# A decoder step on one core: another order of the first loads, of the retrieval of token tiles and of the one-hot work, an earlier read-back, and a split last tile

## The chip, the core and the metric

The kernel runs on one core of a Trainium2 chip. It uses five engines: TensorE (PE, with its weight loads shown apart as PEld), VectorE (DVE), ScalarE (ACT), GpSimd (POOL) and SyncE (SP), which issues most of the DMAs. The metric is the device time of one execution in microseconds (us).

## What is computed

One layer of a decoder for 576 tokens: 512 of a prompt and 64 of a sample group, with 1024 features. A projection feeds windowed attention and a gated spatial branch, both are merged into the residual, then comes a mixture of 16,384 one-neuron experts with product-key retrieval, and a gate over a per-layer embedding.

```python
xn = _rms_norm(x, lp['attn_norm_g'])
z = xn @ lp['w_in']
...
x1 = x + h @ lp['w_out']
x2 = x1 + _peer(_rms_norm(x1, lp['ffn_norm_g']), lp['peer_w_q'], lp['peer_sub_keys'],
                lp['peer_u'], lp['peer_v'])
gate = jax.nn.sigmoid(_rms_norm(x2, lp['ple_norm_g']) @ lp['w_ple_gate'])
x3 = x2 + gate * (p_i @ lp['w_ple'])
...
# _peer, for each token: 8 heads, two halves of a query, top 16 of 128 keys in each half, top 16 of the 256 sums
idx = jnp.take_along_axis(cand_idx, pos, axis=-1)
gate = jax.nn.softmax(best, axis=-1)
act = jax.nn.gelu(jnp.einsum('thkd,td->thk', expert_u[idx], xb))
return jnp.einsum('thk,thkd->td', gate * act, expert_v[idx])
```

## The kernel before

All large products are made in fp32r with both operands split into a high and a low part, so that one block of a product is three matmuls. `split` makes the parts: the high one is an ACT copy (L66), the low one a DVE subtraction (L67). `load_block` reads a block of weights (512 KB), splits it, and gives the split a priority of 1000.

**Head.** `xT[k]`, k = 0 to 7, are the eight blocks of 128 features by 576 tokens. SP loads them, with the first block of `w_in` after the second of them. For each block ACT squares it (L140) and DVE adds the square up (L142), which serves the norm; ACT makes the scaled high part (L181) and DVE the low part (L182). `w_chunk(c, ...)` then multiplies a chunk of 128 columns of `w_in` (48 matmuls, for 256 and 320 tokens) and scales the result with the norm `rn`. The norm's sums over features come from small matmuls (L151, L165) in the same PE queue.

**The five tiles of tokens** are numbered 0 (the 64 sample tokens), 1 to 4 (128 prompt tokens each). `retrieve(ti)` is the top-16 search of one tile, mostly DVE work, a generator that yields between heads. Tiles 0 and 1 fetch their experts' rows from memory (**gather**: L707 on POOL, then DVE L719 and L726). Tiles 2, 3 and 4 (384 tokens) go through **all** experts instead:

- `stage1()` makes one of 128 columns of activations, 24 matmuls of 128x384 against `peer_uT` (L82). 19 of these columns (`SPILL`) are written to memory (`ad`).
- `build_g(tb)`, 24 blocks of 16 tokens, makes the gate of each token as a 128x128 matrix: for each token, a product of two one-hot matrices, `oa` (weights, L822's stationary side) and `ob` (the moving side, 128 columns), both 128x128 in fp32. Four tokens are a group. In even groups ACT makes `oa` and DVE `ob`, one operation of 128x512 (L813). In odd groups, here called mixed ones, DVE makes both: `oa` in one 128x512 compare (L816), `ob` in four operations of 128x128, compare and multiply in one (L819). There are 48 mixed groups. ACT copies the result out of PSUM, and it goes to memory (`gd`).
- `stage2` multiplies the gated activations with `peer_v`: 18 matmuls of 128x512 for each of the 128 columns (L939). Spilled columns are read back as `x1c` from a pool of three buffers, two columns ahead (L946), before DVE multiplies them with the gates (L974) and splits them (L66, L67).

**Order.** The program is written in one order and a scheduler lists each engine's instructions in it, moved by the priorities. SP issues its DMAs in its list's order. `S1_TOPK` says how many columns of stage 1 stand in the retrieval of each tile, `TBK` = 7 at which block of the build the retrieval has to be complete. Before, the tiles 0, 1, 2 are retrieved first, and 3 and 4 step by step inside the build, two steps for each block.

The time from 513.5 to 883.4 us, in which stage 1, the build and the end of retrieval run side by side, is called **phase one** here. Stage 2 follows it.

**Tail.** `finish_tile` makes the last gate of a tile of tokens: 48 matmuls of 128x512 (`tail_gate`, L902) into two PSUM banks that are finished together, then for each half a sigmoid on ACT (L909), a multiplication and an addition on DVE (L910, L911), and a store (`tail_out`).

Of the kernel before, what the change touches and what calls it, by code (L numbers as in the profile page):

```python
# [47 lines left out]
def tile_decoder_step(ctx: ExitStack, tc: tile.TileContext, a, o):  # L48
# [3 lines left out]
    def pool(stack, name, bufs, side="left", **kw):  # L52
        return stack.enter_context(tc.tile_pool(name=name, bufs=bufs, side=side, reuse_waits="tile", **kw))
# [6 lines left out]
    def cload(name, shape, pl=None):  # L60
        t = (pl or const).tile(shape, F32, name="c_" + name, bufs=1)
        S.dma_start(t, a[name])
        return t
# [2 lines left out]
        A.activation(hi, src, AF.Copy)  # L66
        V.tensor_sub(lo, src, hi.bitcast(F32))  # L67

    def load_block(src, shape=(P, KC, P)):
# [4 lines left out]
        with tc.high_priority(offset=1000):  # L74
            split(raw, hi, lo)
        return hi, lo

# [14 lines left out]
    def mm():  # L92
        return psM.tile([P, 512], F32, name="mm")
# [74 lines left out]

    vecs = cload("vecs", [P, 18])
    xT = f8(f4)  # L170
    for k in range(KC):
        S.dma_start(xT[k], a["xT"][k])
        if k == 1:
            first = load_block(a["w_in"][0])
    ident = cload("ident", [P, P])
    xn = (f8(x4), f8(x4))
    tot, add = sumsq()
    for k in range(KC):
        with tc.high_priority(offset=500):
            add(k, xT[k])  # L180
        A.activation(xn[0][k], xT[k], AF.Copy, scale=vecs[:, k:k + 1])  # L181
        V.scalar_tensor_tensor(xn[1][k], xT[k], vecs[:, k:k + 1], xn[0][k].bitcast(F32),  # L182
                               op0=ALU.mult, op1=ALU.subtract)
    rn = e1.tile([P, NT], F32, name="rn", bufs=1)
    with tc.high_priority(offset=500):
        for cols, ps in rstd_rows(tot, lambda: bank("sc")):
# [2 lines left out]
    def w_chunk(c, dst, out):  # L189
        def scaled(ps, cols):  # L190
            with tc.high_priority(offset=1000):
                V.tensor_tensor(dst[:, cols], ps, rn[:, cols], op=ALU.mult)
            out(cols)
        joint(load_block(a["w_in"][c]) if c else first, xn, scaled)

    kraw, vTr = tt(), tt()
    w_chunk(0, kraw, lambda cols: None)
# [584 lines left out]
    def make_ew(e0, e1_, gtf):  # L782
        pt = bank("pt")
        for q, src in enumerate((e1_, gtf, e0)):
            T.transpose(out=pt[:, q * P:(q + 1) * P], in_=src, identity=ident)
        ew = ep.tile([P, 4, P], F32, name="ew")
        A.activation(ew[:, 1:4, :], pt[:, 0:3 * P].rearrange("p (a b) -> p a b", a=3), AF.Copy)
        A.activation(ew[:, 0, :], pt[:, P:2 * P], AF.Copy, scale=-1.0)
        ewT.append(ew)

    found = {}
    tqs.close()
# [2 lines left out]
    ep = pool(gs_s, "ep", 2)  # L795
    op = pool(gs_s, "op", 2)
    gsp = [pool(gs_s, "gsp%d" % i, 1) for i in range(2)]

    def build_g(tb):
        ti, t0 = divmod(tb * TB, P)  # L800
        ew = ewT[ti]
        gs = gsp[(tb + 1) % 2].tile([P, NJ, TB], F32, name="gs")
        for t4 in range(0, TB, 4):
            pt = psB.tile([P, 512], F32, name=("sc", "pt")[t4 // 4 % 2])
            oa = op.tile([P, 4, P], F32, name="oa")
            ob = op.tile([P, 4, P], F32, name="ob")
            c = t0 + t4
            if (tb * TB + t4) // 4 % ONE[1] < ONE[0]:
                for t in range(4):
                    A.activation(oa[:, t, :], iota, AF.Abs, scale=-1.0, bias=ew[:, 3, c + t:c + t + 1])  # L810
                    A.activation(oa[:, t, :], oa[:, t, :], AF.Relu, scale=ew[:, 0, c + t:c + t + 1],
                                 bias=ew[:, 2, c + t:c + t + 1])
                V.tensor_tensor(ob, iota[:, None, :].to_broadcast([P, 4, P]),  # L813
                                ew[:, 1, c:c + 4][:, :, None].to_broadcast([P, 4, P]), op=ALU.is_equal)
            else:
                V.tensor_tensor(oa, iota[:, None, :].to_broadcast([P, 4, P]),  # L816
                                ew[:, 3, c:c + 4][:, :, None].to_broadcast([P, 4, P]), op=ALU.is_equal)
                for t in range(4):
                    V.tensor_scalar(ob[:, t, :], iota, ew[:, 1, c + t:c + t + 1], ew[:, 2, c + t:c + t + 1],  # L819
                                    op0=ALU.is_equal, op1=ALU.mult)  # L820
            for t in range(4):
                T.matmul(pt[:, t * P:(t + 1) * P], lhsT=oa[:, t, :], rhs=ob[:, t, :], start=True, stop=True)  # L822
            A.activation(gs[:, :, t4:t4 + 4], pt.rearrange("p (t j) -> p j t", t=4), AF.Copy)
        if tb == NB // TB - 1:
            A.activation(g0, gs[:, 0:JB, :], AF.Copy)
        S.dma_start(gd[:, :, tb].rearrange("c p j t -> p c (j t)"), gs.rearrange("p (c j) t -> p c (j t)", j=JB))

    for ti in range(3):
        for _ in retrieve(ti, ti < 2):
            if len(acts) < S1_TOPK[ti]:  # L830
                stage1()
        if ti == 0:
            steps.append(gather_steps())
        while len(acts) < S1_TOPK[ti]:
            stage1()
    phase[0] = 1
    rest_t = [retrieve(ti, False) for ti in (3, 4)]
    for tb in range(NB // TB):
        if tb == TBK:
            for i, r_ in enumerate(rest_t):  # L840
                for _ in r_:
                    pass
                make_ew(*found[5 - len(rest_t) + i])
            tks.close()
            late = pool(aLs, "aL", 1, "right")
            acp.append(late.tile([P, RING - NXP, NB], F32, name="aL"))
            g0 = late.tile([P, JB, TB], F32, name="g0")
        if tb < TBK:
            goal = S1_TOPK[2] + (tb + 1) * (S1_PRE - S1_TOPK[2]) // TBK
        else:  # L850
            goal = S1_PRE + (tb - TBK + 1) * (NSP + RING - 1 - S1_END - S1_PRE) // (NB // TB - TBK)
        while len(acts) < goal:
            stage1()
        if tb == 0:
            make_ew(*found[2])
# [49 lines left out]
    def tail_out(x2, r, c0, ps, sg, pl):
        S.dma_start(pl[:r], pld[c0:c0 + r])
        for hh in range(2):
            hs = slice(hh * 512, (hh + 1) * 512)
            A.activation(sg[:r, hs], ps[hh][:r], AF.Sigmoid)  # L909
# [219 lines left out]
```

## Time and profile before

| | us |
|---|---|
| three runs | 1780.88, 1782.16, 1788.48 |
| median | 1782.16 |
| profiled execution, its own time | 1776.88 |
| its span, first to last instruction | 1775.1 |
| PE busy in the span | 1744.3 |
| DVE busy | 1434.0 |
| ACT busy | 867.0 |

The span is what the trace covers; 1.8 us of the execution lie around it. The profiled execution is 5.3 us shorter than the median. PE is busy for 98% of the span, yet its matmuls are pipelined, so a busy PE may still take a longer step from one instruction to the next than it needs.

### The profile page before, as it was taken

To read this page: it belongs to the slowest core of one execution; us is meant where nothing else is said; L and a number is where in the kernel's file an instruction comes from. 1 tells how busy PE (TensorE), PEld (TensorE's weight loads), DVE (VectorE), ACT (ScalarE), POOL (GpSimd) and SP (SyncE) were. 2 spreads that over 40 slices of the span, in tenths; PEclk is the share of its full clock that TensorE was granted. 3 is DMA by queue.
4 is the path that set the end of the run, shared out by engine and by line. 5 is a ranking of instruction groups with operands and counts; after the bars stand their busy time and mean duration, and the time that the engine had idled before them with its cause. 6 is when DMAs were issued, how large, how long until landed. Compare 5 with 4: busy or idle time off the path is not lost.

```text
span 1775.1 us, 27763 instructions
## 1 busy us (share of the span) xinstructions
PE 1744.3 (98%) x10094; PEld 1575.1 (89%) x10094; DVE 1434.0 (81%) x2876; ACT 867.0 (49%) x1525; POOL 525.9 (30%) x390
## 2 busy tenths in 40 slices
PE   7999999999999899999999999999999999999998
PEld 7988999999999899999988887899899899887876
DVE  6455556548999999999898888998888888999862
ACT  6567444343236698999833333333333333333441
POOL 0000000000002112455245554454544554566300
PEclk9999999999999999999999999999999999999999
DMA  7211233443226577999999999999999999999741
GB/s 242 75 60 38 71 105 122 141 152 106 81 92 225 173 244 235 361 350 355 352 388 367 371 388 364 394 410 369 365 338 360 364 334 331 335 379 376 284 132 70
DMA packets 176457, 457.06 MB, mean 257 GB/s; under 512 B 15552, under 2 KB 76736, under 8 KB 174272
## 3 DMA queue, kind: packets, MB, share of 16 engines
q1 hardware_dynamic: 120736, 253.22, 40.6%
q0 software_dynamic: 55584, 202.07, 30.8%
q8 instruction: 79, 1.29, 0.3%
q14 instruction: 58, 0.48, 0.1%
HBM read 420.18 MB, written 35.78 MB: 257 GB/s over the span
## 4 chain that ended last, share of the span: by engine, by line
PE 77%; issue 7%; DVE 6%; DMA 5%; POOL 3%; ACT 1%; SPq 0%; DVEq 0%; POOLq 0%; ACTq 0%
PE mm L82 36%; PE oacc L939 21%; PE pv L82 5%; POOL row L707 3%; PE sc L822 2%; DMA row<-peer_v,idx 2%; PE pt L822 2%; PE oacc L902 2%; DVE w_lo L67 2%; PE sc L82 1%; DMA x1c<-ad 1%; DVE row L719 1%; DMA row<-peer_u,idx 1%; PE sc L580 1%; PE pv L447 1%
## 5 line engine op out<-in xcount | busy, mean ns | idle before, releaser
L66 ACT ACTIVATE w_hi<-w_raw 128x1024 fp32r<-128x1024 f32 x325 | 343.9, 1059 | 372.9 <-PE mm L82 287.1
L707 POOL DMA_INDIRECT row<-peer_u,idx x192 | 261.1, 1360 | 872.0 <-issue 520.8
L67 DVE TENSOR_TENSOR w_lo<-w_raw,w_hi 128x1024 fp32r<-128x1024 f32 x325 | 396.6, 1221 | 74.0 <-ACT w_hi L66 73.7
L82 PE MATMUL mm<-xd,w_hi 128*128 128x384 f32 x1552 | 405.9, 341 | 0.5 <-ACT w_hi L66 0.5
L82 PE MATMUL mm<-x,w_hi 128*128 128x256 f32 (+1 forms) x1600 | 329.7, 300 | 9.8 <-ACT x L181 9.5
L707 POOL DMA_INDIRECT row<-peer_v,idx x192 | 263.3, 1372 | 231.8 <-DVE acc L726 202.8
L82 PEld LDWEIGHTS mm<-xd,w_hi 128*128 128x128 f32 x1552 | 281.6, 189 | 5.9 <-ACT w_hi L66 0.8
L82 PEld LDWEIGHTS mm<-x,w_hi 128*128 128x128 f32 x1600 | 257.8, 190 | 24.1 <-ACT x L181 10.0
L82 PE MATMUL mm<-xd,w_lo 128*128 128x384 f32 x776 | 264.4, 341 | 3.7 <-DVE w_lo L67 3.7
L726 DVE SCALAR_TENSOR_TENSOR acc<-row,wts,acc 128x1024 f32<-128x1024 f32 x192 | 245.8, 1280 | 5.3 <-DMA row<-peer_v,idx 4.9
L939 PE MATMUL oacc<-w_hi,wl 128*128 128x512 f32 x768 | 242.0, 397 | 3.7 <-DVE wl L67 3.6
L939 PE MATMUL oacc<-w_lo,wh 128*128 128x512 f32 x768 | 242.0, 396 | 0.4 <-DVE w_lo L67 0.4
L939 PE MATMUL oacc<-w_hi,wh 128*128 128x512 f32 x768 | 242.3, 396 | 0.0
L719 DVE SCALAR_TENSOR_TENSOR row<-row,xr 128x1024 f32<-128x1024 f32 x192 | 231.6, 1221 | 11.0 <-DMA row<-peer_u,idx 8.6
L82 PE MATMUL mm<-x,w_lo 128*128 128x256 f32 (+1 forms) x800 | 236.6, 296 | 0.0
L939 PEld LDWEIGHTS oacc<-w_hi,wl 128*128 128x128 f32 x768 | 144.3, 188 | 39.6 <-DVE wl L67 5.5
L939 PEld LDWEIGHTS oacc<-w_lo,wh 128*128 128x128 f32 x768 | 144.4, 188 | 35.5 <-DVE w_lo L67 1.7
L939 PEld LDWEIGHTS oacc<-w_hi,wh 128*128 128x128 f32 x768 | 143.7, 188 | 29.4 <-ACT xr L921 0.8
L82 PEld LDWEIGHTS mm<-x,w_lo 128*128 128x128 f32 x800 | 151.7, 190 | 1.1 <-issue 0.8
L82 PEld LDWEIGHTS mm<-xd,w_lo 128*128 128x128 f32 x776 | 147.0, 189 | 4.7 <-DVE w_lo L67 4.7
L82 PE MATMUL pv<-xd,w_hi 128*128 128x384 f32 x496 | 136.7, 348 | 0.7 <-ACT x L776 0.7
L66 ACT ACTIVATE wh<-x 128x384 fp32r<-128x384 f32 x66 | 34.7, 526 | 162.6 <-PE oacc L939 153.1
(304 smaller groups left out, 2308.8 us busy)
## 6 DMA issues: line engine op xcount, KB each, us to landing
w_raw<-peer_uT SPq DMA_DIRECT2D x128, 512.0 KB
w_raw<-peer_v SPq DMA_DIRECT2D x128, 512.0 KB
gd<-gs SPq DMA_DIRECT2D x24, 1024.0 KB
gs<-gd SPq DMA_DIRECT2D x15, 1536.0 KB
w_raw<-w_in SPq DMA_DIRECT2D x30, 512.0 KB
w_raw<-peer_wq SPq DMA_DIRECT2D x16, 512.0 KB
w_raw<-w_br SPq DMA_DIRECT2D x8, 512.0 KB
w_raw<-w_out SPq DMA_DIRECT2D x8, 512.0 KB
```

What stands on the lines that cost most here:

```text
L66: A.activation(hi, src, AF.Copy)
L67: V.tensor_sub(lo, src, hi.bitcast(F32))
L82: mark_pe[0] = T.matmul(ps, lhsT=w[wi][:, wk + k, :], rhs=x[xi][k], start=i == 0, stop=i == n - 1)
L447: T.matmul(ps[:r], lhsT=xi[:, k, :r], rhs=wl_[k][wi][:, hh * 512:(hh + 1) * 512], start=i == 0, stop=i == 5)
L580: T.matmul(ps[:, b * P:(b + 1) * P], lhsT=qp[:, b * P:(b + 1) * P], rhs=sk, start=True, stop=True)
L707: ins = G.indirect_dma_start(out=row_, out_offset=None, in_=table, in_offset=bass.IndirectOffsetOnAxis(ap=ix, axis=0))
L719: V.scalar_tensor_tensor(row_, row_, 1.0, xrs[ti], op0=ALU.mult, op1=ALU.mult, accum_out=dots[:, s:s + 1])
L726: V.scalar_tensor_tensor(accs[ti], row_, wts[:, s:s + 1], accs[ti], op0=ALU.mult, op1=ALU.add)
L822: T.matmul(pt[:, t * P:(t + 1) * P], lhsT=oa[:, t, :], rhs=ob[:, t, :], start=True, stop=True)
L902: T.matmul(ps[hh][:r], lhsT=xi[:, k, :r], rhs=w[k][wi][:, hh * 512:(hh + 1) * 512], start=k == 0 and xi is xh and wi == 0, stop=k == KC - ...
L939: mark_pe[0] = T.matmul(oacc[t][hh], lhsT=wi[:, ts], rhs=vi[:, hh * 512:(hh + 1) * 512], start=j == 0 and last == 0 and vi is vh, stop=j = ...
```

## The change

Five parts. (a) Head: SP loads the first block of `w_in` ahead of the `xT` blocks and the second ahead of the constants; the high and low parts come ahead of the squares; the first chunk goes through k with both halves of the tokens in step, and the first three chunks use banks of three pools. (b) Tiles 0 and 2 are retrieved first, and 3, 1 and 4 inside the build, three steps for each block. (c) In a block of the build, one bf16 compare of 128x1024 (`hot`) serves both mixed groups, and one multiplication of 128x512 makes `ob` from it; in `ob` the four tokens are now innermost, so that the moving side of a matmul takes every fourth element. (d) `x1c` is read back four columns ahead instead of two, from the same three buffers. (e) The tail loads its embedding before the gate's matmuls, and the last tile is done in three groups of columns, 512, 256 and 256, each with its own output.

```diff
-S1_TOPK = (4, 9, 13)
+S1_TOPK = (4, 12)
...
 
     vecs = cload("vecs", [P, 18])
     xT = f8(f4)
+    first = [load_block(a["w_in"][0])]
     for k in range(KC):
         S.dma_start(xT[k], a["xT"][k])
-        if k == 1:
-            first = load_block(a["w_in"][0])
+    first.append(load_block(a["w_in"][1]))
     ident = cload("ident", [P, P])
+    first.append(load_block(a["w_in"][2], urgent=False))
     xn = (f8(x4), f8(x4))
     tot, add = sumsq()
     for k in range(KC):
-        with tc.high_priority(offset=500):
+        with tc.high_priority(offset=1500):
+            A.activation(xn[0][k], xT[k], AF.Copy, scale=vecs[:, k:k + 1])
+            V.scalar_tensor_tensor(xn[1][k], xT[k], vecs[:, k:k + 1], xn[0][k].bitcast(F32),
+                                   op0=ALU.mult, op1=ALU.subtract)
+    with tc.high_priority(offset=500):
+        for k in range(KC):
             add(k, xT[k])
-        A.activation(xn[0][k], xT[k], AF.Copy, scale=vecs[:, k:k + 1])
-        V.scalar_tensor_tensor(xn[1][k], xT[k], vecs[:, k:k + 1], xn[0][k].bitcast(F32),
-                               op0=ALU.mult, op1=ALU.subtract)
...
-        joint(load_block(a["w_in"][c]) if c else first, xn, scaled)
+        w = first[c] if c < 3 else load_block(a["w_in"][c])
+        if c:
+            joint(w, xn, scaled, bk=(mm, lambda: bank("pv"), lambda: bank("pt"))[c] if c < 3 else mm)
+            return
+        pss = [mm()[:, :cols.stop - cols.start] for cols in HALVES]
+        for k in range(KC):
+            for ps, cols in zip(pss, HALVES):
+                for i, (wi, xi) in enumerate(((0, 0), (0, 1), (1, 0))):
+                    T.matmul(ps, lhsT=w[wi][:, k, :], rhs=xn[xi][k][:, cols], start=k == 0 and i == 0,
+                             stop=k == KC - 1 and i == 2)
+        for ps, cols in zip(pss, HALVES):
+            scaled(ps, cols)
...
         ew = ep.tile([P, 4, P], F32, name="ew")
+        ewh = ep.tile([P, P], BF16, name="ewh")
+        A.activation(ewh, pt[:, 0:P], AF.Copy)
         A.activation(ew[:, 1:4, :], pt[:, 0:3 * P].rearrange("p (a b) -> p a b", a=3), AF.Copy)
         A.activation(ew[:, 0, :], pt[:, P:2 * P], AF.Copy, scale=-1.0)
-        ewT.append(ew)
+        ewT.append((ew, ewh))
...
+    hp = pool(gs_s, "hp", 1)
+    iota4 = hp.tile([P, P, 4], BF16, name="iota4")
+    A.activation(iota4, iota[:, :, None].to_broadcast([P, P, 4]), AF.Copy)
...
+        ew, ewh = ewT[ti]
+        hot = hp.tile([P, P, 2, 4], BF16, name="hot")
+        e1c = ewh[:, t0:t0 + TB].rearrange("p (g s t) -> p g s t", g=2, s=2)[:, :, 1, :]
+        V.tensor_tensor(hot, iota4[:, :, None, :].to_broadcast([P, P, 2, 4]),
+                        e1c[:, None].to_broadcast([P, P, 2, 4]), op=ALU.is_equal)
         gs = gsp[(tb + 1) % 2].tile([P, NJ, TB], F32, name="gs")
...
-            if (tb * TB + t4) // 4 % ONE[1] < ONE[0]:
+            cols = [ob[:, t, :] for t in range(4)]
+            if t4 // 4 % 2 == 0:
...
             else:
                 V.tensor_tensor(oa, iota[:, None, :].to_broadcast([P, 4, P]),
                                 ew[:, 3, c:c + 4][:, :, None].to_broadcast([P, 4, P]), op=ALU.is_equal)
-                for t in range(4):
-                    V.tensor_scalar(ob[:, t, :], iota, ew[:, 1, c + t:c + t + 1], ew[:, 2, c + t:c + t + 1],
-                                    op0=ALU.is_equal, op1=ALU.mult)
+                obx = ob.rearrange("p a b -> p (a b)").rearrange("p (x t) -> p x t", t=4)
+                V.tensor_tensor(obx, hot[:, :, t4 // 8, :],
+                                ew[:, 2, c:c + 4][:, None, :].to_broadcast([P, P, 4]), op=ALU.mult)
+                cols = [obx[:, :, t] for t in range(4)]
             for t in range(4):
-                T.matmul(pt[:, t * P:(t + 1) * P], lhsT=oa[:, t, :], rhs=ob[:, t, :], start=True, stop=True)
+                T.matmul(pt[:, t * P:(t + 1) * P], lhsT=oa[:, t, :], rhs=cols[t], start=True, stop=True)
...
-    for ti in range(3):
+    for i, ti in enumerate((0, 2)):
         for _ in retrieve(ti, ti < 2):
-            if len(acts) < S1_TOPK[ti]:
+            if len(acts) < S1_TOPK[i]:
                 stage1()
         if ti == 0:
             steps.append(gather_steps())
-        while len(acts) < S1_TOPK[ti]:
...
     phase[0] = 1
-    rest_t = [retrieve(ti, False) for ti in (3, 4)]
+    rest_t = [(ti, retrieve(ti, ti < 2)) for ti in (3, 1, 4)]
+
+    def rest_step():
+        if next(rest_t[0][1], 1) == 1:
+            ti, _ = rest_t.pop(0)
+            if ti in found:
+                make_ew(*found[ti])
+
...
         while len(acts) < goal:
+            if tb == 0 and len(acts) == goal - 1:
+                make_ew(*found[2])
             stage1()
-        if tb == 0:
-            make_ew(*found[2])
         build_g(tb)
-        for _ in range(2):
-            if rest_t and next(rest_t[0], 1) == 1:
-                rest_t.pop(0)
-                make_ew(*found[4 - len(rest_t)])
+        for _ in range(3):
+            if rest_t:
...
@@ -941,9 +967,10 @@
 
     tails, spp, back = [], [], {}
     for j in range(NJ):
-        if j + 2 in SPILL:
-            back[j + 2] = d3.tile([P, NB], F32, name="x1c")
-            S.dma_start(back[j + 2], ad[sorted(SPILL).index(j + 2)])
+        for jb in (2, 4) if j == 0 else (j + 4,):
+            if jb in SPILL:
+                back[jb] = d3.tile([P, NB], F32, name="x1c")
+                S.dma_start(back[jb], ad[sorted(SPILL).index(jb)])
...
     def finish_tile(i, x2, xh, xl, sg, r, c0):
-        tail_gate(ws, xh, xl, r, banks[i])
-        tail_out(x2, r, c0, banks[i], sg, tw.tile([P, D], F32, name="pl"))
+        pl = tw.tile([P, D], F32, name="pl")
+        S.dma_start(pl[:r], pld[c0:c0 + r])
+        parts = list(zip(banks[i], (slice(0, 512), slice(512, D))))
+        groups = [parts]
+        if i == 4:
+            groups = [parts[:1], [(banks[i][1], slice(512, 768))], [(banks[0][0], slice(768, D))]]
+        for g in groups:
+            tail_gate(ws, xh, xl, r, g)
+            tail_out(x2, r, c0, sg, pl, g)
```

SP, the start of the program: `vecs` are scale constants, `c_92` and `c_93` two buffers of four `xT` blocks each, `w_raw` a block of weights. Before, SP's list starts thus:

```order
L62 DMA c_vecs<-vecs 128x18
L172 DMA c_92<-xT 128x576 x2
L71 DMA w_raw<-w_in 128x1024
L172 DMA c_92<-xT 128x576 x2
L172 DMA c_93<-xT 128x576 x4
L62 DMA c_ident<-ident 128x128
```

The changed kernel, with its own line numbers, starts SP's list thus:

```order
L61 DMA c_vecs<-vecs 128x18
L70 DMA w_raw<-w_in 128x1024
L172 DMA c_92<-xT 128x576 x4
L172 DMA c_93<-xT 128x576 x4
L70 DMA w_raw<-w_in 128x1024
L61 DMA c_ident<-ident 128x128
L70 DMA w_raw<-w_in 128x1024
```

The first block of `w_in` has moved ahead of all eight `xT`, the second ahead of `ident`, and the third is in front of the other constants.

DVE, a block late in the build: `row,dots` are gather's dot products, `w_lo` a split of stage 1. Before, two mixed groups and an even one between them stand thus:

```order
L813 TENSOR_TENSOR ob<-c_iota,ew 128x512
L816 TENSOR_TENSOR oa<-c_iota,ew 128x512
L819 TENSOR_SCALAR ob<-c_iota,ew 128x128 x4
L719 SCALAR_TENSOR_TENSOR row,dots<-row,xr 128x1024 x3
L813 TENSOR_TENSOR ob<-c_iota,ew 128x512
L67 TENSOR_TENSOR w_lo<-w_raw,w_hi 128x1024
L816 TENSOR_TENSOR oa<-c_iota,ew 128x512
L819 TENSOR_SCALAR ob<-c_iota,ew 128x128 x4
```

After the change a whole block, two even and two mixed groups, stands thus:

```order
L822 TENSOR_TENSOR hot<-iota_5616,ewh 128x1024
L836 TENSOR_TENSOR ob<-c_iota,ew 128x512
L66 TENSOR_TENSOR w_lo<-w_raw,w_hi 128x1024
L839 TENSOR_TENSOR oa<-c_iota,ew 128x512
L842 TENSOR_TENSOR ob<-hot,ew 128x512
L732 SCALAR_TENSOR_TENSOR row,dots<-row,xr 128x1024 x2
L836 TENSOR_TENSOR ob<-c_iota,ew 128x512
L839 TENSOR_TENSOR oa<-c_iota,ew 128x512
L842 TENSOR_TENSOR ob<-hot,ew 128x512
```

The four operations of a mixed group's `ob` have become one, and one `hot` of 128x1024 stands at the start of a block.

SP, the start of stage 2: `gd` to `gs` is the read of gates, `peer_v` and `peer_uT` are weights. Before, the first read-backs stand thus:

```order
L946 DMA x1c<-ad 128x384 x2
L71 DMA w_raw<-peer_v 128x1024
L946 DMA x1c<-ad 128x384
L71 DMA w_raw<-peer_uT 128x1024
L966 DMA gs<-gd 128x3072
L71 DMA w_raw<-peer_v 128x1024 x2
L946 DMA x1c<-ad 128x384
L71 DMA w_raw<-peer_uT 128x1024
L966 DMA gs<-gd 128x3072
```

After the change they stand thus:

```order
L973 DMA x1c<-ad 128x384 x3
L70 DMA w_raw<-peer_v 128x1024 x2
L993 DMA gs<-gd 128x3072
L973 DMA x1c<-ad 128x384
L70 DMA w_raw<-peer_uT 128x1024
L70 DMA w_raw<-peer_v 128x1024 x2
L993 DMA gs<-gd 128x3072
L70 DMA w_raw<-peer_uT 128x1024
```

The third read-back now stands with the first two, and the fourth ahead of the next `peer_uT` block: each is one pair of columns earlier.

## Rows read from the trace of the kernel before

**Rows 1.** Page, part 1: busy time and share of the span.

```profile
PE 1744.3 (98%) x10094; PEld 1575.1 (89%) x10094; DVE 1434.0 (81%) x2876; ACT 867.0 (49%) x1525; POOL 525.9 (30%) x390
```

**Rows 2.** Stretches: window, length, busy us (count) of PE, PEld, DVE, ACT, POOL; clock, DMA.

```profile
544.00:690.00 146.00, 138.31 (x831) 133.66 (x830) 143.22 (x465) 110.65 (x206) 25.62 (x20) 0.98 0.71 226
690.00:875.00 185.00, 184.81 (x1230) 176.58 (x1230) 181.27 (x358) 170.75 (x409) 83.25 (x57) 1.00 1.01 346
1075.00:1150.00 75.00, 68.33 (x323) 57.23 (x323) 65.29 (x106) 23.69 (x32) 35.81 (x27) 1.00 0.97 377
```

**Rows 3.** Phase one, line L82 alone: busy PE and PEld, with counts.

```profile
513.50:883.40 369.90, 303.75 (x1507) 260.23 (x1507) 0.99 0.83 278
```

**Rows 4.** Phase one, line L822 alone, same columns.

```profile
513.50:883.40 369.90, 116.20 (x768) 102.90 (x768) 0.99 0.83 278
```

**Rows 5.** Chain in phase one: start us, length us, piece.

```profile
517.94 4.16 PE mm L82 x24
...
696.79 0.89 PE sc L822 x8
```

**Rows 6.** Timeline of DVE, build: start us, us, line, operation.

```profile
745.10 0.68 DVE L813 TENSOR_TENSOR ob<-c_iota,ew 128x512 f32<-128x512 f32 x1
745.71 0.68 DVE L816 TENSOR_TENSOR oa<-c_iota,ew 128x512 f32<-128x512 f32 x1
...
747.44 1.11 DVE L819 TENSOR_SCALAR ob<-c_iota,ew 128x128 f32<-128x128 f32 x4
748.46 0.69 DVE L813 TENSOR_TENSOR ob<-c_iota,ew 128x512 f32<-128x512 f32 x1
```

**Rows 7.** Timeline of DVE, retrieval.

```profile
558.81 1.22 DVE L67 TENSOR_TENSOR w_lo<-w_raw,w_hi 128x1024 fp32r<-128x1024 f32 x1
559.95 0.69 DVE L653 TENSOR_TENSOR l<-pr 128x1024 bf16<-128x1024 bf16 x1
560.55 0.29 DVE L681 TENSOR_REDUCE den<-gate 128x8 f32<-128x128 f32 x1
```

**Rows 8.** Timeline of PE, head.

```profile
9.18 1.44 PE L82 MATMUL mm<-x,w_hi 128*128 128x256 f32 x3 [9.18 <-ACT x L181]
...
12.38 0.41 PE L82 MATMUL mm<-x,w_lo 128*128 128x256 f32 x1
...
12.60 0.47 PE L82 MATMUL mm<-x,w_hi 128*128 128x320 f32 x1
```

**Rows 9.** Chain in the head: start us, length us, piece.

```profile
17.05 1.19 PE sc L151 x12
...
29.52 0.97 PE pv L216 x4
30.49 6.35 PE mm L82 x48
```

**Rows 10.** First 32 us, line L165 alone: busy PE and PEld, with counts.

```profile
0.00:32.00 32.00, 1.80 (x10) 1.46 (x10) 1.00 0.74 260
```

**Rows 11.** Tile x1c, 900 to 1140 us: DVE and ACT idle until (us, times).

```profile
  DMA x1c<-ad: 13.4, 7
```

**Rows 12.** Timeline around two waits in stage 2.

```profile
1081.44 0.56 DVE L974 TENSOR_TENSOR x1c<-x1c,gs 128x384 f32<-128x384 f32 x1 [4.91 <-DMA x1c<-ad]
...
1084.12 0.44 PE L82 MATMUL mm<-xd,w_lo 128*128 128x384 f32 x1 [2.49 <-DVE w_lo L67]
```

**Rows 13.** Timeline a little later.

```profile
1122.56 0.73 PE L939 MATMUL oacc<-w_hi,wl 128*128 128x512 f32 x2 [1.15 <-DVE wl L67]
```

**Rows 14.** Timeline of the end.

```profile
1768.34 0.63 PE L902 MATMUL oacc<-gh,x 128*128 128x512 f32 x2
1768.81 1.08 ACT L909 ACTIVATE xn<-oacc 128x512 f32<-128x512 f32 x2 [10.11 <-issue]
...
1770.65 1.29 DVE L911 TENSOR_TENSOR xn<-xn,x 128x512 f32<-128x512 f32 x2
```

More of the change, by code (lines that the diff above doesn't have):

```diff
@@ L31 @@
 GT = (2.0, 3.5)
-ONE = (1, 2)
 TAIL0 = 112
 TAIL1 = 122
-S1_TOPK = (4, 9, 13)
+S1_TOPK = (4, 12)
 TBK = 7
@@ L67, in split, with load_block @@
         V.tensor_sub(lo, src, hi.bitcast(F32))
-    def load_block(src, shape=(P, KC, P)):
+    def load_block(src, shape=(P, KC, P), urgent=True):
         raw = wp.tile(list(shape), F32, name="w_raw", bufs=4)
@@ L73, in load_block @@
         lo = wp.tile(list(shape), F32R, name="w_lo", bufs=3)
-        with tc.high_priority(offset=1000):
+        with tc.high_priority(offset=1000 if urgent else 0):
             split(raw, hi, lo)
@@ L797, in tile_decoder_step @@
     gsp = [pool(gs_s, "gsp%d" % i, 1) for i in range(2)]
+    hp = pool(gs_s, "hp", 1)
+    iota4 = hp.tile([P, P, 4], BF16, name="iota4")
+    A.activation(iota4, iota[:, :, None].to_broadcast([P, P, 4]), AF.Copy)
     def build_g(tb):
         ti, t0 = divmod(tb * TB, P)
-        ew = ewT[ti]
+        ew, ewh = ewT[ti]
[3 more added lines that the diff above has]
+                        e1c[:, None].to_broadcast([P, P, 2, 4]), op=ALU.is_equal)
         gs = gsp[(tb + 1) % 2].tile([P, NJ, TB], F32, name="gs")
@@ L833, in tile_decoder_step @@
             steps.append(gather_steps())
-        while len(acts) < S1_TOPK[ti]:
+        while len(acts) < S1_TOPK[i]:
             stage1()
     phase[0] = 1
-    rest_t = [retrieve(ti, False) for ti in (3, 4)]
+    rest_t = [(ti, retrieve(ti, ti < 2)) for ti in (3, 1, 4)]
[4 more added lines that the diff above has]
+                make_ew(*found[ti])
     for tb in range(NB // TB):
         if tb == TBK:
[L840 to L843, printed above, removed]
+            while rest_t:
+                rest_step()
             tks.close()
@@ L848, in tile_decoder_step @@
         if tb < TBK:
-            goal = S1_TOPK[2] + (tb + 1) * (S1_PRE - S1_TOPK[2]) // TBK
+            goal = S1_TOPK[1] + (tb + 1) * (S1_PRE - S1_TOPK[1]) // TBK
         else:
@@ L852, in tile_decoder_step @@
         while len(acts) < goal:
+            if tb == 0 and len(acts) == goal - 1:
+                make_ew(*found[2])
             stage1()
-        if tb == 0:
-            make_ew(*found[2])
         build_g(tb)
-        for _ in range(2):
-            if rest_t and next(rest_t[0], 1) == 1:
-                rest_t.pop(0)
-                make_ew(*found[4 - len(rest_t)])
+        for _ in range(3):
+            if rest_t:
+                rest_step()
         pay(GT[tb >= TBK] if tb < 22 else 0)
@@ L896, in tail_scale, with tail_gate, tail_out @@
         V.scalar_tensor_tensor(xn3[:r], x2[:r], ss[:r], pg[:r], op0=ALU.mult, op1=ALU.mult)
-    def tail_gate(w, xh, xl, r, ps):
+    def tail_gate(w, xh, xl, r, parts):
         for k in range(KC):
             for xi, wi in ((xh, 0), (xh, 1), (xl, 0)):
-                for hh in range(2):
-                    T.matmul(ps[hh][:r], lhsT=xi[:, k, :r], rhs=w[k][wi][:, hh * 512:(hh + 1) * 512],
+                for p, hs in parts:
+                    T.matmul(p[:r, :hs.stop - hs.start], lhsT=xi[:, k, :r], rhs=w[k][wi][:, hs],
                              start=k == 0 and xi is xh and wi == 0, stop=k == KC - 1 and xi is xl)
[L905 to L909, printed above, removed]
+    def tail_out(x2, r, c0, sg, pl, parts):
+        for p, hs in parts:
+            A.activation(sg[:r, hs], p[:r, :hs.stop - hs.start], AF.Sigmoid)
             V.tensor_tensor(sg[:r, hs], sg[:r, hs], pl[:r, hs], op=ALU.mult)
```

## The prediction

> **What bounds the kernel now.** I read the page's busy times first: PE is busy for 98% of the span, DVE for 81% [rows 1]. So a gain has to come from a place where PE waits or steps slowly. Next I read busy times by stretch, where three places show. From 544 to 690 us DVE is busy for 143.2 of 146 us and PE for 138.3: DVE's retrieval sets the pace. From 690 to 875 PE counts as busy throughout, with DVE at 181.3 and ACT at 170.8 of 185: three engines close to their limits. From 1075 to 1150, in stage 2, PE idles for 6.67 us [rows 2].
>
> In phase one the PE's busy time hides its losses, so I counted steps. The chain shows 24 matmuls of 128x384 in 4.16 us, 0.173 each, and eight of the build's in 0.89, 0.111 each [rows 5]. Phase one has 1507 and 768 of them [rows 3, 4]: 1507 x 0.173 + 768 x 0.111 = 261 + 85.5 = about 347 us of work in a stretch of 369.9. Some 23 us are lost; 7.7 of it is idle time before 690, the rest mostly longer steps while PE waits for operands.
>
> At the ends PE stands alone. It starts at 9.18 us [rows 8], and after its last matmul a chain of ACT and DVE closes the span [rows 14].
>
> **(a) Head: -3 us.** PE's first step there is slow: the 256-column matmul took 0.22 us (12.38 to 12.60) [rows 8], while 48 matmuls took 6.35 later, 0.132 each [rows 9]; the 320-column one fits, so I use 0.24 for a slow step. The changed order loads the first weights ahead of `xT`, and the high part of `xT` no longer queues behind ACT's squares. I estimate a start at 7.5 instead of 9.18, chosen from the same loads with one square less ahead, and leave the steps slow until 15, as before. That makes 31 steps by 15; the other 17 of the first chunk take 2.2, to 17.2. The second chunk takes 6.35, the norm's small matmuls 1.19 (L151) and 1.80 (L165), the L216 group 0.97 [rows 9, 10]: 27.5. Before, the same work (two chunks, norm, L216) ended at 29.52 + 0.97 = 30.49. So -3, with bounds of -1 (the loads do not come sooner) and -6 (steps quick from the start). That the third chunk too may now begin ahead of the norm only fills gaps: its 48 matmuls are due in either order.
>
> **(b) Order of retrieval: 0.** The same operations move between blocks. DVE is busy for 98% of both stretches [rows 2], so its sum, and not its order, sets the time; the cover is DVE's own queue. If the order itself opened or closed gaps, the 7.7 us of PE idling before 690 [rows 2] bound it either way.
>
> **(c) One-hots: -4 us in phase one.** Before, a mixed group's `ob` took four operations, 1.02 us (747.44 to 748.46); a 128x512 fp32 operation takes 0.61 (745.10 to 745.71) [rows 6]. After it is one such multiplication and half of a bf16 compare of 128x1024. The nearest row is a bf16 operation of that size: 0.60 (559.95 to 560.55), against 1.14 for fp32 (558.81 to 559.95) [rows 7]. At 0.60 the group costs 0.61 + 0.30 = 0.91, and 48 groups save 48 x 0.11 = 5.3 us of DVE. If the compare runs at the fp32 step, it is 0.61 + 0.57 = 1.18 and costs 48 x 0.16 = 7.7 more. I take 0.60, since operands and result are bf16 as in the row. Of the 5.3 I count 4, as DVE is the fullest engine before 690 and PE has losses to give back after it; bounds 0 (ACT and PE bind instead) and -5.3. Three small ACT copies and one 128x512 copy are some 2 us of ACT in 370, at nothing, because ACT has 35 us free before 690 [rows 2].
>
> The build's matmuls are the disputed cost. In mixed groups the moving operand now steps over four fp32 values, 16 bytes; that is 384 of the 768 instructions. No row of before shows such a step. I bound it: below by nothing, above by twice the time, 0.222 for 0.111. I take nothing: PE takes a column in 0.45 ns from the fp32r matmuls (4.16 us / 24 / 384) but in 0.87 ns in the build (0.111 us / 128) [rows 5], so columns can be delivered at twice the rate that the build needs.
>
> [...]
>
> **(d) Read-back: -4 us.** From 900 to 1140 DVE waited 13.4 us in 7 waits for `x1c` [rows 11]. One of them (4.91 us) ends at 1081.44, and the PE stop of 2.49 at 1084.12 lies two operations behind it [rows 12]; another PE stop of 1.15 stands behind a split [rows 13]. Two columns earlier is some 8 us earlier (18 matmuls of 512 columns at 0.45 ns are 4.1 us for a column), more than the longest wait. Bounds: -2.5 (that one stop) and -6.7 (all idling of the stretch); I take the middle, 4, since DVE runs ahead of PE for most of the other waits. What is late next are `w_raw` blocks, as DMA runs at 0.97 of its time there [rows 2]. On SP the read-back waits for its buffer earlier now, with the next `peer_v` load queued behind it; the buffer is that of two columns ago, whose split is done by then.
>
> **(e) Tail: -1.8 us.** From 1768.81 to 1771.94 two sigmoids, two multiplications and two additions end the work: 3.13 us [rows 14]. With a last group of 256 columns, only its own chain stands behind the last matmul. Three operations of 512 columns at the 0.61 of [rows 6] are 1.84, of 256 about half, 0.92. So the saving lies between 1.3 and 2.2; I take 1.8. The 256-column matmuls cost nothing more: a column takes 0.45 ns in either width.
>
> **Sum.** -3 - 4 - 4 - 1.8 = -12.8. Against the profiled execution's own 1776.88 (span 1775.1 and 1.8 around it) that is 1764; that execution stood 5.3 below the median, so on the median of 1782.16 it is 1769. With all bounds at their ends the forecast reaches from 1762 to 1777. A measurement of this kernel can tell about 0.5%, 8.9 us, from no change.
>
> **Rivals.**
>
> A, slower: the strided operand doubles the build's step. 384 x 0.111 = 42.6 us of PE work more, 389 in all, and at least 7 of the 23 lost us remain: 396 for phase one instead of 369.9, +26. With (a), (d), (e) at -8.8 it is +17: 1799. For it: PE is the bound after 690. Against it: the two rates above. It decides from 0.065 us more for each instruction (347 + 7 + 384 x 0.065 = 379, which eats up the other parts' 8.8), and makes the kernel slower by 0.5% from 0.09. A phase one of its own length hides up to 0.03.
>
> B, no change: the compare steps as fp32. DVE gets 7.7 more, of which nearly 7 shows because DVE is full: +7 - 8.8 = -2, 1780. For it: the operands are broadcast in two dimensions, which the row of 0.60 does not have.
>
> C, the change doesn't do what it says at the head and in stage 2: DMA is the limit there (0.97), so that earlier issue lands no sooner. Then only (c) and (e) are left: -5.8, 1776.
>
> D, inside the forecast's range: ACT and PE bind in phase one, and (c) gives nothing: 1773.
>
> **How the numbers follow.** Forecast with D 0.60, A 0.20, B 0.10, C 0.10. The likeliest gives 1769. A's time depends on a price between 0.03 and 0.111, 1773 to 1799, so I reach up to 1797; below, some room under 1762 for the order of retrieval, 1757. Outside are the dearer half of A and both ends of the rest. Faster by over 0.5% (below 1773): most of the forecast, 0.55, and 0.05 of C with a bigger part (c): 0.6. Within 0.5%: B, the rest of C and of the forecast, and the cheap end of A: 0.22. Slower: the dear part of A, 0.18.
>
> **What would show it.** `hot` at a step near 0.60 and `ob` in mixed groups near 0.61 show (c), 1.14 shows B. Eight build matmuls of a mixed group in the chain at 0.89 show that the stride is free; 1.8 shows A, and DVE would then stand idle in phase one. L216 ending near 27.5 shows (a). No DVE waits for `x1c`, and less PE idling from 1075 to 1150, show (d); waits for `w_raw` in their place show C. One to two us from the last matmul to the end of DVE show (e). I am wrong if phase one is not shorter than 369.9 us, or if the tiles' new order leaves DVE idle before 690.

## The result: slower by 1.4%

The changed kernel took 1805.28 us (median of 6 runs, 1802.24 to 1807.49) against 1780.42 for the kernel before in the same runs. The ratio is 1.0136, with a 95% interval of 1.0117 to 1.0156: 24.2 us slower (0.0136 x 1780). The forecast of 1769 and the range up to 1797 both missed; the sign and the size are those of rival A, a little beyond its 1799.

**The profile after.** The page's busy times, as in [rows 1]:

```profile
PE 1782.9 (99%) x10118; PEld 1614.8 (89%) x10118; DVE 1432.0 (79%) x2758; ACT 873.5 (48%) x1530; POOL 520.7 (29%) x390
```

PE gained 38.6 us of busy time, more than the span gained (30.4, from 1775.1 to 1805.5), while DVE stayed where it was. That points at longer PE instructions; which ones, the rows below show. The two profiled executions (1807.31 and 1776.88) lie further apart than the medians (24.9), so some 5 us between the two traces are their own scatter. Next the stretches, as in [rows 2]; phase one now goes from 511.5 us (the first 128x384 matmul of stage 1) to 911.9 (the first of stage 2):

```profile
511.50:911.90 400.40, 396.29 (x2267) 381.90 (x2266) 354.80 (x870) 308.82 (x654) 97.63 (x75) 1.00 0.79 256
1075.00:1150.00 75.00, 75.00 (x360) 65.33 (x359) 67.06 (x109) 26.89 (x36) 38.67 (x27) 1.00 1.01 397
1150.00:1160.00 10.00, 5.78 (x20) 5.32 (x20) 6.95 (x12) 1.58 (x2) 1.36 (x2) 0.67 0.96 374
1155.00:1160.00 5.00, 4.73 (x15) 4.73 (x16) 5.00 (x10) 1.06 (x1) 1.36 (x2) 0.50 0.92 347
```

Phase one takes 400.4 us instead of 369.9. Its DVE was expected to be full, but is busy for 354.8 of the 400.4. From 1075 to 1150 PE no longer idles, as was forecast, but right after, from 1150 to 1160, it is busy for a part of the time only, at a mean granted clock of 0.67, and of 0.50 in the second half. The build's matmuls (L846 now) alone in phase one, as in [rows 4]:

```profile
511.50:911.90 400.40, 153.16 (x768) 131.36 (x768) 1.00 0.79 256
```

Their number is the same and their busy time 153.16 instead of 116.20. The chain in the build, as in [rows 5], gives their steps:

```profile
699.98 0.45 PE sc L846 x4
704.58 1.81 PE pt L846 x8
```

Four matmuls of an even group (bank `sc`) take 0.45 us, 0.111 each; eight of mixed groups (bank `pt`) take 1.81, 0.226 each, where [rows 5] has 0.89. DVE's groups in phase one, by operation (the last numbers are busy us and mean ns of one):

```profile
L842 DVE TENSOR_TENSOR ob<-hot,ew 128x512 f32<-128x512 bf16 x48 | 32.8, 684 | 0.0
L822 DVE TENSOR_TENSOR hot<-iota,ewh 128x1024 bf16<-128x1024 bf16 x24 | 16.4, 685 | 0.0
```

Each mean holds some 0.09 us that overlaps the next operation, as the 0.68 and 0.69 of [rows 6, 7] do beside their steps of 0.61 and 0.60. So both new operations run at the speed that the prediction took. The timeline of stage 2, at the stop after 1150:

```profile
1153.05 1.03 DVE L1001 TENSOR_TENSOR x<-x,gs 128x384 f32<-128x384 f32 x2 [6.74 <-DMA gs<-gd]
...
1155.27 0.69 PE L81 MATMUL mm<-xd,w_lo 128*128 128x384 f32 x1 [4.22 <-DVE w_lo L66]
...
1160.22 0.33 PE L81 MATMUL mm<-xd,w_lo 128*128 128x384 f32 x1
```

DVE waits 6.74 us for `gs`, the read of gates, and PE stops for 4.22 behind it. In [rows 12] it was `x1c`, and 2.49. Last, the end of the span, as in [rows 14]:

```profile
1801.09 0.28 PE L930 MATMUL mm<-gh,x 128*128 128x256 f32 x1
1801.41 0.38 ACT L935 ACTIVATE xn<-mm 128x256 f32<-128x256 f32 x1 [2.38 <-PE mm L930]
1801.83 0.43 DVE L936 TENSOR_TENSOR xn<-xn,pl 128x256 f32<-128x256 f32 x1 [1.87 <-ACT xn L935]
1802.29 0.42 DVE L937 TENSOR_TENSOR xn<-xn,x 128x256 f32<-128x256 f32 x1
```

From the start of the last sigmoid to the end of DVE there are 1.30 us (1801.41 to 1802.71), where it was 3.13.

### The profile page after: what moved, and what is told of

Read it like the earlier page. It is cut to its first block, busy times and chain, and to the rows that moved or that the text cites. A ratio compares the mean times of both kernels' runs of the same rounds, so it can differ in the third digit from the quotient of the medians.

```text
span 1805.5 us, 27714 instructions
## 1 busy us (share of the span) xinstructions
PE 1782.9 (99%) x10118; PEld 1614.8 (89%) x10118; DVE 1432.0 (79%) x2758; ACT 873.5 (48%) x1530; POOL 520.7 (29%) x390
## 4 chain that ended last, share of the span: by engine, by line
PE 89%; DMA 3%; issue 3%; DVE 2%; POOL 2%; ACT 1%; SPq 0%; POOLq 0%; DVEq 0%; ACTq 0%
PE mm L81 40%; PE oacc L965 24%; PE pv L81 7%; PE pt L846 5%; PE sc L846 3%; PE oacc L930 2%; POOL row L720 2%; PE sc L81 1%; DMA row<-peer_v,idx 1%; DMA gs<-gd 1%; DMA row<-peer_u,idx 1%; PE sc L593 1%; PE pv L460 1%; PE mm L930 1%; PE pv L328 1%
## 5 line engine op out<-in xcount | busy, mean ns | idle before, releaser
L720 POOL DMA_INDIRECT row<-peer_u,idx x192 | 255.6, 1331 | 892.0 <-issue 513.3
L81 PE MATMUL mm<-x,w_hi 128*128 128x320 f32 (+1 forms) x1504 | 307.3, 298 | 0.0
L81 PEld LDWEIGHTS mm<-x,w_hi 128*128 128x128 f32 x1504 | 240.6, 189 | 12.5 <-issue 9.0
L81 PE MATMUL mm<-x,w_lo 128*128 128x320 f32 (+1 forms) x752 | 221.4, 295 | 0.0
L81 PEld LDWEIGHTS mm<-x,w_lo 128*128 128x128 f32 x752 | 141.8, 189 | 1.1 <-issue 0.8
```

Of the source, the lines that this page charges most:

```text
L81: mark_pe[0] = T.matmul(ps, lhsT=w[wi][:, wk + k, :], rhs=x[xi][k], start=i == 0, stop=i == n - 1)
L720: ins = G.indirect_dma_start(out=row_, out_offset=None, in_=table, in_offset=bass.IndirectOffsetOnAxis(ap=ix, axis=0))
```

## Experiments

The theory was that the stride of the matmul's moving operand loses the time. The rival was the new order of retrieval. Each run is compared with the kernel before on the same chip; the ratio's 95% interval stands in brackets.

**1. All strides in one kernel.** The kernel before, with only the order of the moving operand's columns changed, in the fp32 matmuls of the build and in some of stage 1's fp32r matmuls. The products' columns come out in another order, so the values differ; the amount of work is the same.

```diff
-T.matmul(pt[:, t * P:(t + 1) * P], lhsT=oa[:, t, :], rhs=ob[:, t, :], start=True, stop=True)
+st = (2, 4, 8, 16, 1, 32)[tb % 6] if t4 // 4 % 2 else 1
+ov = ob[:, t, :].rearrange("p (x s) -> p s x", s=st)
+T.matmul(pt[:, t * P:(t + 1) * P], lhsT=oa[:, t, :], rhs=ov, start=True, stop=True)
...
+if 64 <= j < 88:
+    s_ = (2, 4, 8, 16)[j % 4]
+    xs = tuple([t_[:, :].rearrange("p (x s) -> p s x", s=s_) for t_ in half] for half in xb)
```

> The kernel before, with nothing changed but the order in which PE reads the moving operand: in mixed groups of the build the 128 columns are read with a step of 2, 4, 8, 16, 1 and 32 fp32 values (8 to 128 bytes), one step for a block in turn, and in stage 1 the columns 64 to 87 read their 384 fp32r columns with a step of 2, 4, 8 and 16 in turn. The columns come out in another order, so the values differ; the work is the same. [...] Rival (the order of retrieval and not the stride lost the time): 0.111 and 0.173 throughout.

The chain in the build: start us, length us, piece. The rows are of mixed groups in blocks that are contiguous, then with steps of 128, 8, 16, 32 and 64 bytes:

```profile
750.42 0.89 PE pt L828 x8
...
829.85 1.78 PE pt L828 x8
...
843.03 0.91 PE pt L828 x8
...
852.17 1.81 PE pt L828 x8
...
865.20 1.86 PE pt L828 x8
...
876.57 1.74 PE pt L828 x8
```

Eight fp32 matmuls take 0.89 contiguous and 0.91 at 8 bytes, but 1.81 at 16, 1.86 at 32, 1.74 at 64 and 1.78 at 128. The chain in stage 2, where the fp32r columns of stage 1 are contiguous in the first row, then at 8, 16, 32 and 64 bytes:

```profile
919.81 4.17 PE mm L82 x24
...
932.37 8.24 PE mm L82 x24
949.00 8.32 PE mm L82 x24
965.73 7.79 PE mm L82 x24
981.92 7.84 PE mm L82 x24
```

24 fp32r matmuls take 4.17 contiguous and 7.8 to 8.3 at every step, at 8 bytes already: 0.45 ns a column becomes 0.85 to 0.90. This run with its 24 slowed columns took 1889.76 in its one execution. The stride theory holds, and the two types differ: fp32 pays nothing at 8 bytes and doubles from 16 to 128, fp32r doubles from 8 to 64.

**2. The stride alone, timed.** As above, with a step of four values (16 bytes) in all mixed groups and nothing in stage 1.

> The kernel before with one thing changed: the matmuls of mixed groups read their moving operand with a step of four fp32 values, 16 bytes. No DVE or ACT instruction and no order changes; the columns of the gates come out in another order, so the values differ. Stride theory: 384 x 0.116 = 44 us more PE work in phase one, of which some 10 to 15 are taken by its lost time: 1780 becomes 1808 to 1816. Rival (order of retrieval): 1780.

1815.82 against 1778.39, ratio 1.0203 [1.0178, 1.0228]: 36 us, at the upper end of what was expected. The chain has the pace that run 1 showed at 16 bytes:

```profile
729.33 1.81 PE pt L825 x8
```

No instruction of another engine and no order differs from the kernel before, so the stride by itself costs more than the whole change lost. If the parts add up, what else the change does gains some 12 us together.

**3. and 4. The stride taken out, with the tokens' layout changed by DVE.** The multiplication reads `hot` with a stride (`a_read`), or writes `ob` with one (`a_write`); the matmul reads contiguous columns.

```diff
...
-V.tensor_tensor(obx, hot[:, :, t4 // 8, :], ew[:, 2, c:c + 4][:, None, :].to_broadcast([P, P, 4]), op=ALU.mult)
+V.tensor_tensor(ob, hot[:, :, t4 // 8, :].rearrange("p x t -> p t x"),
+                ew[:, 2, c:c + 4][:, :, None].to_broadcast([P, 4, P]), op=ALU.mult)          # a_read
+V.tensor_tensor(ob.rearrange("p t x -> p x t"), hot[:, :, t4 // 8, :],
+                ew[:, 2, c:c + 4][:, None, :].to_broadcast([P, P, 4]), op=ALU.mult)          # a_write
...
```

> The changed kernel with ob of mixed groups laid out token by token again, so that the matmul's moving operand is contiguous; the multiplication reads hot with a step of 16 bytes instead. Stride theory: phase one falls from 400 us to 365 to 372 and the kernel to about 1770 if the multiplication still takes 0.60 us; if reading bf16 at that step doubles it to 1.2, DVE gets 29 us more and the time is 1785 to 1795. Rival (order of retrieval): 1805 still.

> As the run before it, but the multiplication goes through hot in its own order and writes ob with a step of 512 bytes, four tokens in turn. Stride theory: about 1770 if the write costs DVE nothing (0.60 us), 1785 to 1795 if it doubles the operation. Rival (order of retrieval): 1805 still.

`a_read` took 1783.61, ratio 1.0025 [1.0013, 1.0037], and `a_write` 1780.73, ratio 1.0001 [0.9985, 1.0017]. Both are 20 us and more faster than the changed kernel, so the rival falls as the whole cause. They do not reach 1770, since the stride's price went to DVE. Its group where it reads with a stride:

```profile
L841 DVE TENSOR_TENSOR ob<-hot,ew 128x512 f32<-128x512 bf16 x48 | 51.5, 1072 | 0.0
```

And where it writes with one:

```profile
L841 DVE TENSOR_TENSOR ob<-hot,ew 128x512 f32<-128x512 bf16 x48 | 51.9, 1081 | 0.0
```

The mean is 1.07 and 1.08 us instead of 0.68, so the operation did not double: 48 x 0.39 = 19 us more DVE work, and times between the two expected. A stride of 16 bytes in bf16 reads and one of 512 bytes in fp32 writes cost the same.

**5. Two tokens innermost.** In run 1 a step of 8 bytes cost the fp32 matmul next to nothing: 0.91 us for eight against 0.89.

```diff
-hot = hp.tile([P, P, 2, 4], BF16, name="hot")
+hot = hp.tile([P, 2, 2, P, 2], BF16, name="hot")
...
+e1c = ewh[:, t0:t0 + TB].rearrange("p (g s q t) -> p g s q t", g=2, s=2, q=2)[:, :, 1]
+for g in range(2):
+    V.tensor_tensor(hot[:, g], iota2[:, None].to_broadcast([P, 2, P, 2]),
+                    e1c[:, g][:, :, None, :].to_broadcast([P, 2, P, 2]), op=ALU.is_equal)
...
+cols = [obx[:, t // 2, :, t % 2] for t in range(4)]
```

> The changed kernel with two tokens innermost instead of four, so that the matmul steps over 8 bytes; the compare is made in two operations of 128x512 for a block. The run with steps of 2 to 32 showed 0.112 us at 8 bytes for the fp32 matmul and 0.227 from 16 on. So if the stride is the whole loss and a short innermost run does not slow DVE (0.30 for each compare, 0.60 for the multiplication): 1778 less what the other parts give, 1765 to 1772. If DVE slows to twice on runs of two: 48 x 0.9 us more DVE work, 1785 to 1795. Rival (the order of retrieval loses part of it): 1780 or more even with DVE's steps short.

1766.29, ratio 0.9927 [0.9911, 0.9942]: 13 us faster than before, and by the two ratios some 37 faster than the changed kernel. DVE's two groups stay quick on runs of two:

```profile
L843 DVE TENSOR_TENSOR ob<-hot,ew 128x512 f32<-128x512 bf16 x48 | 32.9, 685 | 0.1
L823 DVE TENSOR_TENSOR hot<-iota,ewh 128x512 bf16<-128x512 bf16 x48 | 18.5, 417 | 0.0
```

The chain in its build has the contiguous pace, 0.91 for eight:

```profile
715.63 0.91 PE pt L848 x8
```

**6. Tokens outermost, compare kept.** `iotah` holds the numbers 0 to 127 once, in bf16, and `ob` is written token by token, as before the change.

```diff
...
+V.tensor_tensor(hot, iotah[:, None, None, :].to_broadcast([P, 2, 4, P]),
+                e1c[:, :, :, None].to_broadcast([P, 2, 4, P]), op=ALU.is_equal)
...
```

> The changed kernel with tokens outermost, as in the kernel before, but with the shared bf16 compare kept: its second operand is then one value for 128 columns, and everything the matmul reads is contiguous. If the compare still takes 0.60 us for 1024, a mixed group's ob costs 0.90 and the time is that of the run with pairs, 1765 to 1772. If it steps as fp32 does (1.14): 1.17 for a group, 13 us more DVE work than at 0.90, and 1774 to 1782.

1779.83, ratio 1.0003 [0.9990, 1.0015], in the second range:

```profile
L822 DVE TENSOR_TENSOR hot<-iotah,ewh 128x1024 bf16<-128x1024 bf16 x24 | 29.3, 1222 | 0.0
```

With one value for 128 columns as its second operand the compare takes 1.22 us instead of 0.685. So rival B's price exists, in the layout that the change avoided.

**7. The order of retrieval alone**, from the diff of the change.

> The kernel before with the new order of retrieval alone (tiles 0 and 2 first, then 3, 1, 4 inside the build, three steps a block). Stride theory: the order is worth between nothing and a few us in either direction, 1774 to 1782. Rival (order loses time): 1790 or more.

1785.26, ratio 1.0035 [1.0021, 1.0049]: 6 us slower, neither of the two. What DVE waited for in stage 2, from 883 to 1150 us (total us, times, longest), and then PE:

```profile
DVE x1c L978 <- DMA x1c<-ad: 18.2, 8, 3.4
DVE x L978 <- DMA gs<-gd: 7.0, 1, 7.0
PE mm L82 <- DVE w_lo L67: 7.8, 2, 5.2
```

The matmuls of stage 2 begin at 882.63 us here and at 883.34 before, the first of phase one at 512.35 and 513.5, so phase one has kept its length (370.3 and 369.8). What is lost is lost after it: from there to the end of the span are 900.8 us, where it was 891.8. New in it are one wait of 7.0 us for `gs`, behind which PE stops for 5.2 us, and more waiting for `x1c` than in [rows 11]. Behind that stop the granted clock is low as well, as in the changed kernel:

```profile
1130.00:1140.00 10.00, 8.35 (x30) 8.02 (x31) 10.00 (x16) 2.50 (x3) 4.38 (x3) 0.66 0.96 343
```

**8. The earlier read-back alone.**

> The kernel before with the read-back of x1c four columns ahead, alone. If the late x1c is the reason for PE's stops from 1075 to 1150, they go and the kernel gains 2.5 to 6.7 us: 1772 to 1776. If the DMA is full there and the wait only moves to the read of gates, as the changed kernel's trace looks: a gain of 0 to 2 us, 1776 to 1778, and a DVE wait for gs behind which PE stops.

1772.26, ratio 0.9958 [0.9945, 0.9972]: 7 us faster, with an interval from 5 to 10. The same view of DVE's waits:

```profile
DVE x1c L975 <- DMA x1c<-ad: 8.0, 4, 3.6
DVE x L975 <- DMA gs<-gd: 0.9, 1, 0.9
```

The stretch of [rows 2], begun at 1000 us, in the kernel before and then here:

```profile
1000.00:1150.00 150.00, 143.32 (x682) 122.65 (x681) 133.43 (x196) 50.66 (x68) 75.06 (x56) 1.00 0.97 377
1000.00:1150.00 150.00, 147.87 (x712) 128.38 (x712) 136.64 (x202) 51.95 (x69) 75.62 (x54) 1.00 1.00 388
```

DVE waits 8.0 us for `x1c`, not 13.4 as in [rows 11], and PE is busy for 147.87 of 150 instead of 143.32. The wait does not move to `gs` (0.9 us). That it did so in the changed kernel is then a matter of the order of retrieval: all six traces with the new order (the changed kernel and runs 3 to 7) have one wait of 6.2 to 8.0 us for `gs` there, and of the other timed versions none has one over 1.0. SP's reads of gates in the changed kernel:

```profile
1121.32 0.33 SPq L993 DMA_DIRECT2D gs<-gd  x1
...
1128.89 0.33 SPq L993 DMA_DIRECT2D gs<-gd  x1
...
1137.40 0.33 SPq L993 DMA_DIRECT2D gs<-gd  x1
```

And in the kernel with the read-back alone:

```profile
1088.42 0.33 SPq L967 DMA_DIRECT2D gs<-gd  x1
...
1095.71 0.42 SPq L967 DMA_DIRECT2D gs<-gd  x1
...
1118.80 0.33 SPq L967 DMA_DIRECT2D gs<-gd  x1
...
1145.67 0.33 SPq L967 DMA_DIRECT2D gs<-gd  x1
```

Both have two reads of 1.5 MB some 7 us apart. In the changed kernel a third follows 8.5 us later, issued at 1137.40, and the wait for `gs` ends at 1153.05; with the read-back alone the third follows after 23 us. The other new-order traces have the third read within 10 us as well, and their wait ends 15 to 17 us after it. Why the new order's list puts the reads so close was not traced.

**9. Pairs and the old order of retrieval together**, run 5 with the loops and `S1_TOPK` of the kernel before.

> The changed kernel with pairs of tokens innermost (8 bytes) and with the old order of retrieval (tiles 0, 1, 2 first, then 3 and 4, two steps a block). The new order alone made the kernel before 6 us slower, all of it in stage 2, where DVE waited longer for x1c and for gs. If that cost stands beside the earlier read-back too, this version is at 1757 to 1762, faster than the 1766 with the new order. Rival (the earlier read-back already removes what the order costs): 1764 to 1768.

1762.90, ratio 0.9909 [0.9888, 0.9931]. It is the fastest version here, 17 us under the kernel before, and lies between the two expectations. By the medians the order costs 3.4 us beside the earlier read-back (1766.29 against 1762.90, 5 runs each, taken on two chips); the intervals of the two ratios overlap, so the size is not shown. The traces agree with a cost: from 1000 to 1150 PE is busy for 148.94 us here and for 144.85 with the new order. The waits, first with the new order (run 5; DVE, then PE), then here:

```profile
DVE x L1003 <- DMA gs<-gd: 7.7, 2, 6.9
PE mm L81 <- DVE w_lo L66: 5.2, 1, 5.2
DVE x L999 <- DMA gs<-gd: 0.9, 1, 0.9
```

**10. to 12. The other parts alone**, each from the diff (one-hots in pairs).

> The kernel before with the one-hot part alone, two tokens innermost instead of four. If the prediction's step for the one-hots holds once the stride is free: DVE saves 5.3 us, phase one 4, so 1775 (1773 to 1779). Rival (PE and ACT bind in phase one): 1779.

> The kernel before with the new order of the head alone. The prediction said 3 us less, and the changed kernel's first stage-1 matmul of 384 tokens came at 511.5 instead of 513.5: 1776 to 1777. Rival (DMA at the head is full, nothing is gained): 1779.

> The kernel before with the new tail alone. The prediction said 1.8 us less, and the changed kernel's last matmul lies 4.2 us before the end of the span instead of 6.1: 1777. Rival (the smaller groups cost PE what the chain saves): 1779.

One-hots 1776.28, ratio 0.9991 [0.9977, 1.0004], which cannot tell a gain of 4 us from none. Phase one is 4.0 us shorter in its trace (365.84 against 369.84), but it is 374.20 in that of the tail, which changes nothing there, so the trace does not settle it. Head 1774.61, ratio 0.9979 [0.9966, 0.9992]: 3.7 us. Tail 1777.51, ratio 0.9984 [0.9969, 0.9999]: 2.8 us, hardly above what the runs can tell.

## Why the prediction was wrong

**The step that failed** is the price of the strided operand in (c): "I take nothing", because PE takes a column in 0.45 ns in fp32r and in 0.87 in the build, "so columns can be delivered at twice the rate that the build needs." The two rates of [rows 5] are right, but both are of contiguous columns, and the first does not survive a stride: run 1 has fp32r at 0.85 to 0.90 ns a column from 8 bytes on. Nor does fp32r's rate say what fp32 pays: at 8 bytes fp32 kept its pace (0.89 ns a column), and at 16 it went to 1.77, though fp32r's 0.85 to 0.90 would still about cover its 0.87. Why the two types differ no run shows.

The upper bound of the same step, 0.222 us for each of 384 instructions, was twice the contiguous 0.111 by my own estimate, with no row behind the factor; it is what came (0.226), and rival A's place and price were right: 384 x 0.115 = 44 us more PE work. Alone (run 2) it makes phase one 38.2 us longer (513.84 to 921.92 in its trace), in the changed kernel 30.5, with the other parts beside it. That the missing 6 us of run 2 fell into the time that PE had been losing there is argued and not shown. The chance of 0.20 for A was the misjudgement, and its upper end was cut off the range.

**The other terms, by the runs.**

| part | predicted us | alone, us | in the profile after |
|---|---|---|---|
| (a) head | -3 | -3.7 | first stage-1 matmul 2.0 earlier |
| (b) order | 0 | +6.2 | new wait for `gs` in stage 2 |
| (c) one-hots, no stride | -4 | -1.6, unclear | DVE steps as predicted |
| (c) stride | 0 | +36 | 0.226 us a matmul |
| (d) read-back | -4 | -7.5 | no stop at 1075 to 1150, one after it |
| (e) tail | -1.8 | -2.8 | chain 1.8 shorter |

The parts alone sum to +26.6, against the 24.2 measured; each is known to some 2 us, the stride to 4. Without the stride the time came out near the predicted sum of -12.8: run 5 gained 13. That is in part luck, since the order cost something that was put at nothing and the read-back gave more than its 4; the parts alone without the stride sum to -9.4.

- (a) The size was right, the place not. PE began at 6.42 us and was through the first chunk near 17.0, not far from the 7.5 and 17.2 of the prediction. The L216 group (L229 now) was to end near 27.5. It ended at 32.08 (31.09 + 0.99), later than the 30.49 of [rows 9], since the squares and their sums now come last and the norm's small matmuls start at 22.87 instead of 17.05; the chain of the changed kernel:

```profile
22.87 1.26 PE sc L150 x12
...
31.09 0.99 PE pv L229 x4
```

PE spent the waiting time on the third chunk, which I had said "only fills gaps". The gain is in PE's busy time of the first 50 us, in the kernel before:

```profile
0.00:50.00 50.00, 40.15 (x274) 37.73 (x275) 29.22 (x44) 30.00 (x54) 1.48 (x6) 1.00 0.70 228
```

And in the changed kernel, 2.2 us more:

```profile
0.00:50.00 50.00, 42.38 (x294) 40.42 (x295) 30.52 (x46) 32.30 (x57) 1.49 (x6) 1.00 0.70 228
```

In the traces of the other versions with the new head, phase one begins 4.1 to 5.5 us earlier than before (at 508.20 with the head alone), so the changed kernel's one trace, with 2.0, shows less of this gain than they do.

- (b) That DVE's "sum, and not its order, sets the time" held for phase one and not for the whole kernel: with the new order SP's reads of gates stand closer together, in a stretch where DMA is at 0.97 of its time before [rows 2] and at 1.01 in the profile after, and one of them comes late in every trace of that order (run 8).
- (d) came out larger than the 4: 7.5 us, with an interval from 5 to 10 that still holds the bound of 6.7. From 1000 to 1150 PE got back 4.6 us (147.87 against 143.32); where the rest came from was not traced. In the changed kernel the wait took another form, as rival C had said of a late transfer in its place (there `w_raw`, here `gs`). The PE stop of 4.22 us was followed by a granted clock of 0.50 from 1155 to 1160, where it was 1.00 from 1075 to 1150 [rows 2], around the stop of 2.49 us of [rows 12]. At 0.50 the 15 matmuls of 128x384 from 1155.27 to 1160.22 took 4.95 us, 0.33 each against the 0.173 of [rows 5], so some 2.4 us were lost beside the stop; that the stop lowered the clock was not shown.
- (c) on DVE: rival B did not come; both steps were those of the rows taken.

## What to carry to other kernels

Before a layout is chosen for the engine that writes a tile, price the engine that reads it: here some 5 us of DVE work were saved for 44 us of PE work. A rate measured on contiguous data is no evidence on strided data (fp32r went from 0.45 ns a column to 0.85 to 0.90), and where a price is unknown between nothing and twice, the bound with 40 us behind it deserves more than a fifth of the chance. A smaller innermost run, two values instead of four, served both engines here: 0.91 us for eight matmuls, 0.685 for a multiplication.

## What was unexpected of the hardware

- The moving operand's step costs an fp32 matmul nothing at 8 bytes (0.91 us for eight against 0.89) and doubles it from 16 to 128 bytes (1.74 to 1.86); it doubles an fp32r matmul at 8 bytes already (8.24 us for 24 against 4.17).
- On DVE a 128x512 multiplication takes 1.07 us with a 16-byte step in its bf16 input and 1.08 with a 512-byte step in its fp32 output, against 0.68; runs of two values cost nothing (0.685).
- A bf16 compare of 128x1024 takes 0.685 us where both inputs have runs of four values, and 1.22 where one input is a single value for 128 columns.
